# First tile of an FFN up projection: eight plain products instead of seven combined ones, with the combinations made meanwhile

## The chip, the cores and the metric

The kernel runs on one NeuronCore of one Trainium2 chip, as one program. Five engines have queues of their own: TensorE (PE in the profile; PEld are its weight loads), VectorE (DVE), ScalarE (ACT), GpSimd (POOL) and SyncE (SP, which here only issues DMAs). Each takes its instructions in a fixed order; semaphores make one wait for another. The metric is the time of one execution on the device in microseconds, median of several runs. Lower is better.

## What is computed

An encoder layer of width 1024 for 1024 "prompt" tokens and 256 "sample" tokens: a token mixing block, cross-attention into 256 memory tokens, and a gated feed-forward network (FFN), each with a root mean square norm in front and a residual sum behind. The change lies where the attention's output projection ends and the FFN begins:

```python
def rmsnorm(x, w):
    xf = x.astype(jnp.float32)
    y = xf * lax.rsqrt(jnp.mean(xf * xf, -1, keepdims=True) + EPS)
    return (y * w.astype(jnp.float32)).astype(x.dtype)
...
    return o @ w_o
...
    x = x + memory_cross_attention(rmsnorm(x, norm_xa_w), rmsnorm(mem, norm_mem_w), xa_w_q, xa_w_kv, xa_w_o)
    h = rmsnorm(x, norm_ffn_w)
    gu = h @ ffn_w_gate_up
    x = x + (jax.nn.silu(gu[..., :D_FF]) * gu[..., D_FF:]) @ ffn_w_down
```

Here D_FF is 2816, all tensors are float32.

## The kernel before

**Layout and precision.** Activations lie feature-major: 128 partitions, KT = 8 slices of features, tokens along the free dimension. Tokens form three blocks (`BLOCKS`): 0 and 1 are the prompt's halves of 512 tokens, 2 is the sample's 256. Every float32 product is made of three matmuls in the float32r type: `split` (line 124) writes a high part on ScalarE (line 125) and the remainder, the low part, on VectorE or GpSimd (line 126); `mm3` (line 110) issues high x high, high x low and low x high. So one 128-feature slice of a product costs three matmuls of 512 columns, or of 256 for the sample.

**Order of the work.** TensorE runs in the program's order, as the generators yield it. The other engines' instructions are ordered by the tile framework: by the order in the program and by when their inputs are ready, so that they may be placed well ahead of where the source has them; once built, each engine's order is fixed. Side jobs (`K.side`) are generators that wake when a clock has passed a due time. That clock is counted by hand in `mm` (line 100): a matmul of n columns adds n / 2.4 ns. A norm (`Norm.rest`, line 252) is such a job: after `lag` it sends a first few small matmuls (sums over partitions of the squares in `nacc`), then VectorE makes the inverse root (`nst`, lines 224 to 228), after `lag2` a few more small matmuls spread it, and then every `pace` one of 8 slices is scaled (line 284) and handed to a `sink`, which splits it.

**Output projection** (`OutProj.run`, line 1227). Eight weight tiles m, blocks b. Tiles 0 and 1 go first for all blocks, then block 0, 1 and 2 in turn with m = 2 to 7. `evac` (line 1237) adds the residual into x[b] and feeds the norm. After a block's last m its x is stored to `x2d`, and its norm is started as a side job. After block 0 `first_weights` loads the raw weights of the first up tile. The six weight tiles from m = 2 on lie in a pool of six rooms (`wx2`), closed when the projection ends.

**FFN up stage.** 22 tiles f of 128 gate and 128 up columns. For the prompt a seven-product (Strassen and Winograd) scheme is used for the pair gate and up over two halves of features and two halves of tokens. b11 and b21 are the feature halves of block 0, b12 and b22 of block 1. The combinations, made once and used by all tiles, are

    r1 = b11 - b12,  r2 = -b22 - r1,  t3 = b22 - b12,  t4 = -r2 - b21

and per tile four weight forms of 1024 columns: w(0) the gate weights, w(1) the first sums (`gu_sa`), w(2) the second sums (`gu_sb`), w(3) the up weights. A product, `gu_mm` (line 1570), is four slices, 12 matmuls of 512 columns. `sample` does the sample with plain weights in halves of 12 matmuls of 256 columns. `ff_up` (line 1757) is one tile: seven products, four half samples, gating, and stores for the down stage.

`ff_first` (line 1717) is tile 0. In it, block 1's sink has already formed r1 and r2 as the norm went along, slice by slice (lines 1427 and 1431); t3 and t4 are made between the products (`make_t3`, `make_t4`) in eight slices of 512 columns. Tile 0's combined weights are formed on VectorE within the projection. Tile 1's weights are loaded within `ff_first` (lines 1724 and 1741), two products of tile 1 are moved up into tile 0 to fill a gap, and block 2's norm is late (`LAGS` 19000, `LAGS2` 8000), so that the sample of tile 0 is done within tile 1.

## Time and profile before

| | |
|---|---|
| median of three runs | 2257.43 us (2254.76 to 2261.45) |
| the profiled execution | 2255.0 us |
| its span, first to last instruction | 2253.2 us |
| instructions in the trace | 32407 |
| matmuls, busy time of TensorE | 12468, 2196.2 us (97%) |
| VectorE, ScalarE, GpSimd busy | 1394.0, 815.5, 532.7 us |
| mean granted clock of TensorE | 0.993 |

Times in the profile's views are microseconds from the start of the span. Matmuls overlap, so the rate of TensorE is read from the distance of their starts. A wait is shown as the idle time of an engine ahead of an instruction, with the instruction whose end released it. "L284" is line 284 of the kernel; helpers such as line 126 serve many tiles, which the names before the arrow tell apart. In a groups row, after the bar, stand busy time, mean of one in ns, and idle time before them. In a waits row stand the total, how often, and the longest. In a windows row stand the length, then for each engine busy time and number of instructions, then the granted clock, the DMA share and the rate.

### The profile page before, as it was taken

To read this page: it belongs to the slowest core of one execution; us is meant where nothing else is said; L and a number is where in the kernel's file an instruction comes from. 1 tells how busy PE (TensorE), PEld (TensorE's weight loads), DVE (VectorE), ACT (ScalarE), POOL (GpSimd) and SP (SyncE) were. 2 spreads that over 40 slices of the span, in tenths; PEclk is the share of its full clock that TensorE was granted. 3 is DMA by queue.
4 is the path that set the end of the run, shared out by engine and by line. 5 is a ranking of instruction groups with operands and counts; after the bars stand their busy time and mean duration, and the time that the engine had idled before them with its cause. 6 is when DMAs were issued, how large, how long until landed. Compare 5 with 4: busy or idle time off the path is not lost.

```text
span 2253.2 us, 32407 instructions
## 1 busy us (share of the span) xinstructions
PE 2196.2 (97%) x12468; PEld 1918.3 (85%) x12468; DVE 1394.0 (62%) x2770; ACT 815.5 (36%) x1481; POOL 532.7 (24%) x355
## 2 busy tenths in 40 slices
PE   6999999999999999999999999899999999999998
PEld 6988888888888898888888888688888888888888
DVE  7768788887985964664534537544334334568575
ACT  5434243433424433233343423323232323243453
POOL 3010000000000000013231331565666566300031
PEclk9999999999999999999999999999999999999999
DMA  5221322223234445962231431223222222493531
GB/s 185 83 79 68 104 69 87 77 69 95 73 111 125 159 140 165 305 236 94 84 106 45 157 143 57 75 76 110 87 82 76 88 76 82 136 363 126 198 111 57
DMA packets 191301, 262.47 MB, mean 116 GB/s; under 512 B 72410, under 2 KB 102698, under 8 KB 191146
## 3 DMA queue, kind: packets, MB, share of 16 engines
q1 hardware_dynamic: 171306, 231.30, 30.9%
q10 hardware_dynamic: 19840, 29.11, 3.5%
q8 instruction: 97, 1.59, 0.3%
q14 instruction: 58, 0.48, 0.1%
HBM read 182.19 MB, written 78.16 MB: 116 GB/s over the span
## 4 chain that ended last, share of the span: by engine, by line
PE 82%; DVE 8%; issue 4%; DMA 2%; ACT 2%; POOL 1%; SPq 0%; POOLq 0%; ACTq 0%; DVEq 0%
PE bank L108 81%; PE bank L121 1%; DMA tbd<-stage 1%; DVE acc L599 1%; DVE wlo L126 1%; DMA t<-sgd 1%; DVE nt L284 1%; DVE U L845 0%; DVE sw L903 0%; DVE lo L126 0%; DMA stage<-gtd 0%; DVE W L745 0%; DVE nacc L249 0%; DVE aT L714 0%; DVE zt L837 0%
## 5 line engine op out<-in xcount | busy, mean ns | idle before, releaser
L108 PE MATMUL bank<-hi,whi 128*128 128x512 f32 (+1 forms) x2144 | 763.3, 356 | 2.8 <-ACT whi L125 1.7
L108 PE MATMUL bank<-lo,whi 128*128 128x512 f32 (+1 forms) x2144 | 748.8, 349 | 1.1 <-POOL lo L126 1.1
L108 PE MATMUL bank<-hi,wlo 128*128 128x512 f32 (+1 forms) x2144 | 748.3, 349 | 0.9 <-DVE wlo L126 0.9
L108 PEld LDWEIGHTS bank<-hi,wlo 128*128 128x128 f32 x2144 | 406.0, 189 | 54.9 <-DVE wlo L126 1.3
L108 PEld LDWEIGHTS bank<-hi,whi 128*128 128x128 f32 x2144 | 406.9, 190 | 52.7 <-ACT whi L125 2.2
L108 PEld LDWEIGHTS bank<-lo,whi 128*128 128x128 f32 x2144 | 407.1, 190 | 49.8 <-POOL lo L126 1.4
L126 POOL TENSOR_TENSOR wlo<-raw,whi 128x1024 fp32r<-128x1024 f32 x70 | 177.8, 2542 | 377.2 <-ACT whi L125 377.2
L125 ACT ACTIVATE whi<-raw 128x1024 fp32r<-128x1024 f32 (+1 forms) x141 | 144.5, 1026 | 195.3 <-PE bank L108 146.9
L126 POOL TENSOR_TENSOR wlo<-room,whi 128x1024 fp32r<-128x1024 f32 x42 | 100.6, 2396 | 115.7 <-ACT whi L125 115.7
L108 PE MATMUL bank<-bhl,whi 128*128 128x512 f32 x408 | 125.7, 389 | 0.0
L126 DVE TENSOR_TENSOR wlo<-raw,whi 128x1024 fp32r<-128x1024 f32 (+1 forms) x71 | 82.3, 1159 | 43.6 <-ACT whi L125 41.5
L125 ACT ACTIVATE whi<-room 128x1024 fp32r<-128x1024 f32 x42 | 44.6, 1061 | 142.5 <-PE bank L108 138.6
L1796 DVE TENSOR_TENSOR room<-room,bank 128x512 f32<-128x512 f32 x21 | 14.5, 688 | 131.8 <-ACT room L1567 131.8
L108 PEld LDWEIGHTS bank<-bhl,whi 128*128 128x128 f32 x408 | 76.5, 188 | 15.9
L599 DVE SCALAR_TENSOR_TENSOR acc<-craw,sm,acc 128x510 f32<-128x510 f32 (+1 forms) x96 | 73.6, 766 | 20.5 <-ACT acc L597 19.0
L108 PE MATMUL bank<-bhl,wlo 128*128 128x512 f32 x204 | 79.5, 390 | 1.2 <-DVE wlo L126 1.2
L745 DVE TENSOR_TENSOR W<-W,UT 128x2 f32<-128x2 f32 (+30 forms) x155 | 73.2, 472 | 10.1 <-DMA W<-in_eye 5.8
L248 ACT ACTIVATE nsq<-x 128x512 f32<-128x512 f32 (+1 forms) x70 | 40.2, 583 | 102.7 <-DVE x L1237 92.4
L962 ACT ACTIVATE gs<-bank 128x512 f32<-128x512 f32 (+1 forms) x60 | 31.2, 520 | 125.2 <-PE bank L108 119.9
L1589 DVE SCALAR_TENSOR_TENSOR t<-bank,t 128x512 f32<-128x512 f32 (+1 forms) x44 | 24.6, 558 | 82.2 <-PE bank L108 82.2
L249 DVE TENSOR_TENSOR nacc<-nacc,nsq 128x512 f32<-128x512 f32 (+1 forms) x72 | 54.4, 755 | 33.2 <-ACT nsq L248 31.9
L108 PE MATMUL bank<-bhl,ahl 128*128 128x512 f32 x312 | 73.8, 392 | 0.0
(345 smaller groups left out, 4223.1 us busy)
## 6 DMA issues: line engine op xcount, KB each, us to landing
raw<-in_w_gu SPq DMA_DIRECT2D x44, 512.0 KB, 3.9
braw<-gq SPq DMA_DIRECT2D x14, 1024.0 KB, 5.4
raw<-in_w_g SPq DMA_DIRECT2D x20, 512.0 KB, 3.3
gq<-t SPq DMA_DIRECT2D x33, 256.0 KB, 2.0
gtd<-gs ACTq DMA_DIRECT2D x32, 256.0 KB, 2.0
w<-in_w_dn SPq DMA_DIRECT2D x8, 1024.0 KB, 11.9
raw<-in_w_qkv SPq DMA_DIRECT2D x12, 512.0 KB, 3.6
gq<-r SPq DMA_DIRECT2D x22, 256.0 KB, 4.3
```

The lines of the kernel that those rows point to most:

```text
L108: self.nc.tensor.matmul(out, l, r, start=start, stop=stop, skip_group_check=more)
L121: self.nc.tensor.transpose(out, x, ident)
L125: self.nc.scalar.activation(hi, src, AF.Copy)
L126: (eng or self.nc.vector).tensor_tensor(out=lo, in0=src, in1=f32(hi), op=ALU.subtract)
L248: S.activation(sq, x, AF.Square)
L249: (eng or V).tensor_tensor(out=self.acc, in0=self.acc, in1=sq, op=ALU.add)
L284: V.scalar_tensor_tensor(out=t, in0=xk(k), scalar=sm[:, wcol + k : wcol + k + 1], in1=pb[:, :n], op0=ALU.mult, op1=ALU.mult)
L599: V.scalar_tensor_tensor(out=dst, in0=src, scalar=wj, in1=dst, op0=ALU.mult, op1=ALU.add)
L745: V.tensor_tensor(out=t3, in0=u3[:, i:, c:].rearrange("p j c -> p c j"), in1=XL[:, 32 * i + i : 32 * i + 32].unsqueeze(1).to_broadcast([P, ...
L962: S.activation(t, ps, AF.Tanh, scale=0.5)
L1589: V.scalar_tensor_tensor(out=out, in0=u, scalar=sign, in1=t, op0=ALU.mult, op1=ALU.mult)
L1796: V.tensor_tensor(out=c22, in0=c22, in1=pe, op=ALU.add)
```

## The change

- Tile 0 no longer uses the seven-product scheme. Gate and up are each made by four plain products (b11, b21 for block 0; b22, b12 for block 1): eight products. The copies and sums that put the seven products together go.
- Tile 0's sample is done at the end of tile 0, and tile 1 becomes an ordinary tile.
- Block 1's sink only splits. Its slices come in the order 4 to 7, 0 to 3; slices 0 to 3 (b12) go to rooms of their own. `PACES` and `LAGS2` set the pace of each block's slices (600, 1300, 600) and the second lag (2800, 9500, 7000); the first lag is 1500 for all.
- r1, r2, t3 and t4 are made during the plain products, in operations on two slices (1024 columns) at a time.
- The rooms of the projection's weights m = 2 to 7 are reused one by one as its last block goes (`after(m)`): tile 1's gate and up weights, then b12 (later t3), then r2.
- Tile 1's raw weights are loaded during the projection, after tile 0's were split; its sums are made in place on GpSimd after m = 3 of the last block.
- In all tiles the gate and up weights keep one fixed room each, and the two sums rotate in the two rooms of `wp`.

The core of the diff:

```diff
+                    if b == 2 and after is not None:
+                        after(m)
...
-                if sinks is None or b == 2:
-                    norm_b = nms[b].rest(xk, wcol, to_h(hs, b), 600, lag=1500 if sinks is None else LAGS, inplace=sinks is not None, ready=ready, lag2=2800 if sinks is None else LAGS2)
+                if sinks is None:
+                    norm_b = nms[b].rest(xk, wcol, to_h(hs, b), 600)
                 else:
-                    norm_b = nms[b].rest(xk, wcol, sinks(b, x, hs), (600, PACE1)[b], inplace=True)
+                    norm_b = nms[b].rest(xk, wcol, sinks(b, hs), PACES[b], ks=range(KT) if b != 1 else SECOND_KS, inplace=True, lag2=LAGS2[b])
...
+    SECOND_KS = (4, 5, 6, 7, 0, 1, 2, 3)
...
         def sink(k, t):
-            if k < 4:
-                V.tensor_tensor(out=x0[:, k, :], in0=x0[:, k, :], in1=t, op=ALU.subtract)
-                split(hi[:, k, :], lo[:, k, :], x0[:, k, :], V)
-            else:
-                r2_raw.append(bank())
-                V.scalar_tensor_tensor(out=r2_raw[k - 4], in0=t, scalar=-1.0, in1=x0[:, k - 4, :], op0=ALU.mult, op1=ALU.subtract)
-                split(hi[:, k, :], lo[:, k, :], t, V)
+            h, l = (b12[0][:, k, :], b12[1][:, k, :]) if k < 4 else (hi[:, k, :], lo[:, k, :])
+            split(h, l, t, V)
...
     def gu_gate(f, eng=G):
         if f < NFF:
-            gu_w[f, 0] = pair_of(wp)
+            gu_w[f, 0] = gu_w[1, 0]
...
+        if f == 1:
+            split(hi[:, :512], lo[:, :512], g[:, :512], V)
+            split(hi[:, 512:], lo[:, 512:], u[:, 512:], V)
+            return
...
-        gu_w[f, 2] = pair_of(tpool)
+        hi, lo = gu_w[f, 2] = pair_of(wp)
...
     def gu_up(f):
-        gu_w[f, 3] = pair_of(tpool)
+        gu_w[f, 3] = gu_w[1, 3]
...
+        def splits():
             yield FIRST_W
...
+            for i in (0, 3):
+                gu_w[0, i] = pair_of(wp)
+                split(*gu_w[0, i], gu_raw[0][i // 3], G)
+            gu_load(1, wp)
...
+    def after(m):
+        room = tuple(tpool.tile([P, 1024], F32R, tag=t, name=t) for t in ("whi", "wlo"))
+        if m > 3:
+            for x, t in zip(b12 if m < 6 else r2, room):
+                x.parts.append(t.rearrange("p (k t) -> p k t", t=512))
+            return
+        gu_w[1, 0 if m == 2 else 3] = room
+        split(*room, gu_raw[1][m - 2], G)
+        if m == 3:
+
+            g, u = gu_raw[1]
+            for x, y in ((u[:, 512:], u[:, :512]), (u[:, :512], g[:, :512]), (g[:, :512], u[:, 512:]), (g[:, 512:], g[:, :512])):
+                G.tensor_tensor(out=x, in0=x, in1=y, op=ALU.add)
...
+    def make_r1():
+        for i in (0, 2):
+            V.tensor_tensor(out=room[:, i : i + 2, :], in0=room[:, i : i + 2, :], in1=x1[:, i : i + 2, :], op=ALU.subtract)
+        parts(r1, room)
+
+    def make_r2():
+
+        for i in (0, 2):
+            a, b = x1[:, i : i + 2, :], x1[:, 4 + i : 6 + i, :]
+            V.tensor_tensor(out=a, in0=b, in1=a, op=ALU.subtract)
+            V.scalar_tensor_tensor(out=b, in0=b, scalar=-1.0, in1=room[:, i : i + 2, :], op0=ALU.mult, op1=ALU.subtract)
+        parts(r2, x1[:, 4:, :])
+
+    def make_t34():
+        nonlocal fp
+        for i in (0, 2):
+            x = room[:, 4 + i : 6 + i, :]
+            V.scalar_tensor_tensor(out=x, in0=x1[:, 4 + i : 6 + i, :], scalar=-1.0, in1=x, op0=ALU.mult, op1=ALU.subtract)
+        parts(t3, x1)
         xhs.close()
...
+        parts(t4, room[:, 4:, :])
...
+        gate, up_ = gu_w[0, 0], gu_w[0, 3]
+        pa, pu, pb, pv = (bank(pm) for _ in range(4))
+        for ps, w in ((pa, gate), (pu, up_)):
+            yield from gu_mm(ps, w, 0, b11, True)
+            yield from gu_mm(ps, w, 1, b21, False)
+            if ps is pa:
+                t1 = silu2(pa)
+        times_up(t1, pu, store1(0), 1.0)
+        K.finish(K.pending.pop((id(h3), 1)))
+        yield from gu_mm(pb, gate, 1, b22, True)
+        yield from gu_mm(pb, gate, 0, b12, False)
+        t2 = silu2(pb)
+        make_r1()
+        yield from gu_mm(pv, up_, 1, b22, True)
+        yield from gu_mm(pv, up_, 0, b12, False)
+        c22 = ff(x2p, "nacc", "c22", bufs=2)
+        times_up(t2, pv, store2(0), 1.0, c22)
+        make_r2()
+        K.finish(K.pending.pop((id(h3), 2)))
+        smp.extend(half(h3[2], i) for i in range(2))
+        sg, su = (bank()[:, :NS] for _ in range(2))
+        yield from sample(sg, gate, (0, 1))
+        gu_sa(1)
+        ts_ = silu2(sg, NS)
+        make_t34()
+        yield from sample(su, up_, (0, 1))
+        times_up(ts_, su, gsd[0], 1.0)
         pending["last"] = 0, t1, c22
...
-LAGS, LAGS2, FIRST_W = 19000, 8000, 9000
-PACE1 = 1900
+FIRST_W, PACES, LAGS2 = 9000, (600, 1300, 600), (2800, 9500, 7000)
```

More of the change, by code (lines that the diff above doesn't have):

```diff
@@ L1225, in begin, with run @@
                 yield from self.parts(m, b, range(KT - 2))
-        def run(self, xsrc, scale, wcol, xpool, store, sinks=None, then=None, ready=None):
+        def run(self, xsrc, scale, wcol, xpool, store, sinks=None, then=None, after=None):
             ps = (xpool,) * 3 if sinks is None else (x0p, xhp, xpool)
@@ L1561, in sum_room, with copied @@
         return room[:, i : i + 2, :].rearrange("p a b -> p (a b)")
-    def copied(ps, t=None):
+    def copied(ps, t=None, first=False):
         if t is None:
             turns["p"] += 1
-            t = room[:, 4 + turns["p"] % 2, :]
+            t = room[:, (0 if first else 4) + turns["p"] % 2, :]
         S.activation(t, ps, AF.Copy)
@@ L1717, in ff_first @@
     def ff_first():
-        w = lambda i: gu_w[0, i]
-        pb, pf, pe, pa = (bank(pm) for _ in range(4))
-        cs = first_copies
-        raw = K.raw()[:, :1024]
-        SY.dma_start(raw, a["w_gu"][1])
-        gu_raw[1] = [raw]
-        yield from gu_mm(pb, w(0), 1, b21, True)
-        yield from gu_mm(pa, w(0), 0, b11, True)
-        p1 = copied(pa, cs[:, 0, :])
-        t1 = gate_of(pb, p1)
-        yield from gu_mm(pe, w(1), 1, r1, True)
-        yield from gu_mm(pa, w(1), 0, r2, False)
@@ L1732, in ff_first @@
-        gu_gate(1, V)
-        make_t3()
-        yield from gu_mm(pf, w(2), 1, b22, True)
-        u2 = copied(pa, cs[:, 1, :])
-        V.tensor_tensor(out=u2, in0=u2, in1=pe, op=ALU.add)
-        t2 = gate_of(pf, u2)
-        make_t4()
-        split(*gu_w[0, 3], gu_raw[0][1], V)
-        raw = K.raw()[:, :1024]
-        SY.dma_start(raw, a["w_gu"][NFF + 1])
-        gu_raw[1].append(raw)
-        make_room()
-        pn = bank(pm)
-        yield from gu_mm(pn, gu_w[1, 0], 0, b11, True)
-        pn2 = bank(pm)
@@ L1747, in ff_first @@
-        first_out.extend((pn, pn2))
-        yield from gu_mm(pn2, gu_w[1, 0], 1, b21, True)
-        yield from gu_mm(pa, w(2), 0, t3, False)
-        c22 = copied(pa, second_block(0))
-        V.tensor_tensor(out=c22, in0=c22, in1=pe, op=ALU.add)
-        times_up(t2, c22, store2(0), -1.0, c22)
-        yield from gu_mm(pa, w(3), 1, t4, False)
-        times_up(t1, pa, store1(0), -1.0)
+        gate, up_ = gu_w[0, 0], gu_w[0, 3]
[5 more added lines that the diff above has]
+                t1 = silu2(pa)
@@ L1759, in ff_up @@
         second, last = f == 1, f == NFF - 1
-        sums = lambda: (bank()[:, :NS], bank()[:, :NS])
-        if second:
-            pa, pb = first_out
-            p1 = copied(pa)
-            t1 = gate_of(pb, p1)
-            combine(*pending["last"])
-            K.finish(K.pending.pop((id(h3), 2)))
-            smp.extend(half(h3[2], i) for i in range(2))
-            sg0, su0 = sums()
-            yield from sample(sg0, gu_w[0, 0], (0, 1))
-            gu_sa(1)
-            ts0 = silu2(sg0, NS)
-            sg, su = sums()
-            yield from sample(su0, gu_w[0, 3], (0, 1))
-            times_up(ts0, su0, gsd[0], 1.0)
-        else:
-            pa, pb = bank(pm), bank(pm)
-            yield from gu_mm(pa, w(0), 0, b11, True)
-            p1 = copied(pa)
-            sg, su = sums()
-            yield from sample(sg, w(0), (0,))
-            yield from gu_mm(pb, w(0), 1, b21, True)
-            t1 = gate_of(pb, p1)
-            combine(*pending["last"])
+        pa, pb = bank(pm), bank(pm)
+        yield from gu_mm(pa, w(0), 0, b11, True)
+        p1 = copied(pa, None, second)
+        sg, su = (bank()[:, :NS] for _ in range(2))
+        yield from sample(sg, w(0), (0,))
+        yield from gu_mm(pb, w(0), 1, b21, True)
+        t1 = gate_of(pb, p1)
+        combine(*pending["last"])
         gu_sb(f)
         gu_load(f + 1, wp if f % 2 == 0 else x2p)
-        yield from sample(sg, w(0), (0, 1) if second else (1,))
+        yield from sample(sg, w(0), (1,))
         yield from gu_mm(pa, w(1), 0, r2, False)
-        u2 = copied(pa)
-        gu_up(f)
+        u2 = copied(pa, None, second)
+        if not second:
+            gu_up(f)
         if last:
```

77 lines of the change are left out of this document (25 added, 52 removed).

## Prediction

> **What bounds the kernel now.** I read the page first. The profiled execution took 2255.0 us, of which the span is 2253.2, so 1.8 us lie around it; the three timed runs have a median of 2257.43, which is 2.4 above. The sum below is made against 2255.0 and then carried over to 2257.4.
>
> ```profile
> span 2253.2 us, 32407 instructions
> PE 2196.2 (97%) x12468; PEld 1918.3 (85%) x12468; DVE 1394.0 (62%) x2770; ACT 815.5 (36%) x1481; POOL 532.7 (24%) x355
> ...
> raw<-in_w_gu SPq DMA_DIRECT2D x44, 512.0 KB, 3.9
> ```
>
> TensorE is busy 97% of the span: a change pays only where TensorE waits, and costs wherever it adds matmuls. So I looked next for the waits of TensorE in the stretch that the diff touches. It begins where the output projection has issued its last product (1397.52 us, below called Z) and ends where up tile 2 starts (1464.04 us). The waits view for TensorE over exactly that stretch:
>
> ```profile
> PE bank L108 <- DVE nst L228: 4.3, 1, 4.3
> PE bank L108 <- ACT whi L125: 1.7, 1, 1.7
> PE bank L108 <- POOL lo L126: 1.1, 1, 1.1
> PE bank L108 <- ACT hi L125: 1.0, 1, 1.0
> PE bank L108 <- DVE wlo L126: 0.9, 1, 0.9
> PE bank L108 <- DVE r2l L126: 0.8, 1, 0.8
> PE bank L108 <- ACT room L1567: 0.7, 1, 0.7
> PE bank L108 <- DVE x L1547: 0.6, 1, 0.6
> ```
>
> These add up to 11.1 us, and all are waits for operands being prepared: nst is the third token block's normalisation, whi and wlo are tile 1's gate weights, r2l a combination of activations. The windows view shows the same by tens of us:
>
> ```profile
> core 0: us, PE busy (x) PEld busy (x) DVE busy (x) ACT busy (x) POOL busy (x), PEclk, DMA share, GB/s
> 1378.08:1397.52 19.44, 19.26 (x161) 19.08 (x160) 14.65 (x36) 5.64 (x12) 0.00 (x0) 1.00 0.29 109
> 1397.52:1464.04 66.52, 55.45 (x274) 45.92 (x273) 41.55 (x77) 27.00 (x45) 30.08 (x20) 0.92 0.23 79
> ...
> 1410.00:1420.00 10.00, 6.77 (x30) 4.76 (x30) 10.00 (x17) 6.08 (x10) 0.00 (x0) 1.00 0.14 52
> ...
> 1430.00:1440.00 10.00, 4.76 (x19) 4.17 (x20) 8.31 (x16) 4.27 (x9) 8.16 (x7) 0.54 0.33 105
> ```
>
> In 1410 to 1420 VectorE is busy all of the 10 us while TensorE works 6.77: VectorE limits there. In 1430 to 1440 TensorE is down to 4.76 and the granted clock to 0.54, so after the 4.3 us wait the matmuls also run slowly for a while.
>
> **What the stretch would take without waits.** From the groups by form and the timeline of TensorE:
>
> ```profile
> L108 PE MATMUL bank<-hi,whi 128*128 128x512 f32 x32 | 12.7, 397 | 1.7 <-ACT whi L125 1.7
> ...
> L108 PE MATMUL bank<-hi,whi 128*128 128x256 f32 x32 | 10.1, 317 | 1.0 <-ACT hi L125 1.0
> ```
>
> ```profile
> 1397.52 0.40 PE L108 MATMUL bank<-hi,whi 128*128 128x512 f32 x1
> ...
> 1409.54 0.39 PE L108 MATMUL bank<-hi,whi 128*128 128x512 f32 x1
> ...
> 1412.03 0.39 PE L108 MATMUL bank<-hi,wlo 128*128 128x512 f32 x1
> ...
> 1441.45 0.28 PE L108 MATMUL bank<-lo,whi 128*128 128x256 f32 x1
> ...
> 1447.33 0.28 PE L108 MATMUL bank<-hi,wlo 128*128 128x256 f32 x1
> ...
> 1464.04 0.39 PE L108 MATMUL bank<-hi,whi 128*128 128x512 f32 x1
> ```
>
> The starts, not the durations, give the rate, since matmuls overlap. 1409.54 and 1412.03 are the first and the last of the 12 matmuls of one product: 2.49 / 11 = 0.227 us each, 2.72 us a product. 1441.45 to 1447.33 spans 49 steps of 256 columns: 0.12 us each, 1.44 us for a half sample (12 matmuls). In this stretch the code has 14 products (seven for each of tiles 0 and 1) and 8 half samples: 38.1 + 11.5 = 49.6 us. The third block's norm puts 4 + 4 small matmuls in: the stretch before (first row of the windows, 19.44 us) has 144 steps of 0.12, 17.3 us, and 16 such small ones, so 2.1 / 2 = 1.0 us for eight. So 50.6 of 66.5 us are work, and 15.9 us are lost: the 11.1 of waits, the slow clock, and refilling after each wait.
>
> **The change, part by part.** *TensorE.* Tile 0 takes eight products for seven: +2.72 us, on the path. All else stays: 15 products, 8 half samples, the norm's matmuls, 40.8 + 11.5 + 1.0 = 53.3 us. If no wait were left the stretch would gain 66.5 - 53.3 = 13.2 us. This is the ceiling.
>
> *Waits that go.* Tile 1's gate and up weights are loaded in the second block's products and split from the third block's on; the gate's 1.7 and 0.9 go. The two loads (3.9 us each) move ahead of Z on SP's queue, past the second block's store, which stands behind them; their cover is the second block, 144 matmuls of 0.227 or 32.7 us, in place of two waits for them. Tile 1's sums go from after 1426 to POOL before Z. The first eight products need only plain activations: block 1's have been ready long before Z, so 4 products, 10.9 us, run with nothing to wait for; then b22 and b12, due at Z + 10.9 and Z + 13.6. Block 2's norm is scaled from 1.5 + 9.5 us on the schedule after its last product, where block 3 takes 15.4 (144 times 256 / 2.4 ns); so it begins 4.4 before Z there, 4.9 at the trace's 0.12.
>
> *The third block's norm.* It moves from 19 us after its last product to the default 1.5, and its second half from 8.0 to 7.0 later. It thereby gets new waits: TensorE takes instructions in order, so behind the norm's first matmul all the plain products queue. That matmul needs the last sum of squares:
>
> ```profile
> 1379.73 0.69 DVE L249 TENSOR_TENSOR nacc<-nacc,nsq 128x512 f32<-128x512 f32 x1 [0.76 <-ACT nsq L248]
> ...
> 1401.06 0.42 DVE L249 TENSOR_TENSOR nacc<-nacc,nsq 128x256 f32<-128x256 f32 x1
> ...
> 1424.57 0.16 DVE L266 TENSOR_SCALAR bank<-bank 128x2 f32<-128x2 f32 x1
> ...
> 1432.96 0.15 DVE L228 SCALAR_TENSOR_TENSOR nst<-bank,nst 128x2 f32<-128x2 f32 x1
> ```
>
> With VectorE full (second row) the sum stood 4.0 us after its block's last product at 1397.5; with VectorE idle (first row; products ended 1378.1) 2.3 us. It will be asked for at about 1.6 us (the schedule counts 512 / 2.4 ns = 0.213 us a matmul where the trace has 0.227, so its 1.5 is 1.6 and its 7.0 is 7.4): a wait of 0.7 to 2.4. VectorE will be busy with block 2 again, but with two operations a slice, no longer three: I take 1.7. The chain to nst took 8.5 us between the last two rows, among long operations; it now has 7.4 us, and block 2's last slices are through by about Z + 8, after which nothing urgent is in its way: 0 to 4.3, and I take 0.3.
>
> *VectorE.* Prices, from the groups by form between 1340 and 1470 (the last three are POOL's):
>
> ```profile
> L284 DVE SCALAR_TENSOR_TENSOR x<-x,sm,bank 128x512 f32<-128x512 f32 x16 | 11.3, 741 | 0.0
> L126 DVE TENSOR_TENSOR lo<-x,hi 128x512 fp32r<-128x512 f32 x12 | 9.2, 770 | 0.9 <-ACT hi L125 0.9
> ...
> L126 DVE TENSOR_TENSOR wlo<-raw,whi 128x1024 fp32r<-128x1024 f32 x3 | 3.7, 1218 | 0.0
> L284 DVE SCALAR_TENSOR_TENSOR x<-x,sm,bank 128x256 f32<-128x256 f32 x8 | 3.4, 473 | 1.3 <-PE bank L108 1.3
> ```
>
> ```profile
> L126 POOL TENSOR_TENSOR wlo<-raw,whi 128x1024 fp32r<-128x1024 f32 x10 | 24.9, 2491 | 32.6 <-ACT whi L125 32.6
> ...
> L1475 POOL TENSOR_TENSOR room<-raw 128x512 f32<-128x512 f32 x3 | 4.1, 1382 | 63.5 <-DMA raw<-in_w_gu 63.5
> ...
> L126 POOL TENSOR_TENSOR lo<-x,hi 128x256 fp32r<-128x256 f32 x4 | 3.4, 882 | 0.0
> ```
>
> Due before tile 1's second kind of product (r2): block 2's norm 8 x (0.74 + 0.77) = 12.1; block 3's 12 x 0.47 = 5.7; its chain of eleven at 0.16, 1.8; the last two evacuations with their sums, 4 at 0.42, 1.7; gating of tiles 0 and 1, sums of weights and one combination, 9 x 0.74 + 2 x 0.47 = 7.6; r1 four and r2 six wide operations at 1.22, 12.2. Sum 41.1 us. It may start at Z - 4.9 and is due after 10 products, 6 half samples and the norm, Z + 36.9, or Z + 38.9 with the 2.0 of waits: 43.8 us, 2.7 to spare. The t3 that follows wants 4 wide ones and a half sum, 5.6 us, where TensorE gives 5.4, so what is late for r2 stays late once, not twice. POOL can eat the spare:
>
> ```profile
> 1467.93 2.86 POOL L126 TENSOR_TENSOR wlo<-raw,whi 128x1024 fp32r<-128x1024 f32 x1
> ```
>
> ```profile
> 1468.56 2.78 DVE L1618 SCALAR_TENSOR_TENSOR r<-r,room 128x512 f32<-128x512 f32 x1
> ```
>
> A VectorE operation of 0.74 took 2.78 beside a POOL one, and ended 0.55 after it: it was held until POOL was done. POOL's work for tile 1 (two splits of 2.49, four sums of 1.38, 10.5 us) has the 14 us before Z; its tail may reach past Z - 4.9, and four small splits of block 3 follow. I take 1.2 us of lateness, of 0 to 8.7 (see the first rival).
>
> [...]
>
> *The end of the up stage.* The sums of weights now rotate through the rooms in which gate and first sum rotated. In the last tile, the second room for the down stage's operand 1 is therefore read until the last product; before it was free three products earlier.
>
> ```profile
> 1970.19 2.31 DVE L126 TENSOR_TENSOR wlo<-araw,whi 128x1024 fp32r<-128x1024 f32 x1
> ```
>
> ```profile
> 1972.56 0.50 PE L108 MATMUL bank<-bhl,wlo 128*128 128x512 f32 x1 [1.21 <-DVE wlo L126]
> ```
>
> VectorE already makes TensorE wait 1.21 there, and gets one more wide operation (1.22) ahead of it: 0 to 2.4, I take 0.7. Tiles 2 to 20 have the same rooms' life and no TensorE wait now: nothing.
>
> **Sum.** Stretch 53.3 + 1.7 + 0.3 + 1.2 = 56.5 against 66.5: -10.0; down +0.7; net -9.3. 2255.0 becomes 2245.7, and the median 2257.4 becomes 2248.1.
>
> **Rivals.** *VectorE becomes the bound (0.22).* If all of POOL's work that can fall in the window, four sums 5.5, one split 2.5 and block 3's four 3.4, holds VectorE off, then 11.4 us less the 2.7 to spare are 8.7 us late: stretch 53.3 + 2.0 + 8.7 = 64.0, net -1.8, 2255.6. For it: the two rows above. Against it: most of POOL's work lies where VectorE has gaps, and the L284 operations (one input in PSUM, 741 ns even among POOL's) are not held.
>
> *The wait for nst only moves (0.12).* The norm of block 3 now falls in VectorE's busiest part. With 2.4 + 4.3 us and the slow clock again, the first 18 of its half-sample matmuls at 0.21 for 0.12 (1.8), it is 8.5 instead of 2.0: net -2.8, 2254.6. Here the wait of 1.7 in 1410 to 1420 left the clock at 1.00 and the one of 4.3 did not.
>
> [...]
>
> *Slower (0.08).* If VectorE is held off for 13 us between Z - 5 and Z + 45, nothing is gained (13.2 - 2.0 - 0.7 + 2.7 = 13.2), and from 20 us on a loss is seen. Of its two-input operations there, 8 lo slices, 16 wide ones and 4 halves of sums, each would have to lose about 1 us: 28 - 2.7 + 2.0 + 0.7 - 13.2, or +15 us, 2272. It needs POOL at work in most of that stretch, where it has 11.4 us by count.
>
> **How the numbers follow.** A measurement of this kernel tells about 0.3% (6.8 us) from no change. The forecast has 0.58 with its own range 2244 to 2251, the ends being no wait at all (-13.2) and nearly double the waits (-6). Some 0.05 of it, above 2250.6, counts as no change, and some 0.07 of the two rivals with 0.34 comes out better than -6.8: faster 0.58 - 0.05 + 0.07 = 0.60, same 0.34 - 0.07 + 0.05 = 0.32, slower 0.08. The range for 8 in 10 goes from 0.7 below the ceiling's 2244.2, for the scatter of a median, to just past the first rival: 2243.5 to 2256.
>
> **What would show it.** In the profile after: stretch from the last projection product to tile 2 of 55 to 58 us; 12 more matmuls; no TensorE wait for whi, wlo or t4's source there; one of 1 to 2 us for nacc soon after Z; granted clock 1.00 throughout. Wrong would be: a wait for nst of over 3 us with a clock near half (second rival); waits for r2l, t3l or lo with two-input VectorE operations of 2 us and more (first and third); a gap at 1970 longer by over 2 us; or any new wait before Z.

## The result and the profile after

The changed kernel took 2241.66 us (median of four runs, 2239.54 to 2244.17) beside 2256.1 us for the kernel before (four runs, 2252.9 to 2261.45): a ratio of 0.9934, 95% interval 0.9911 to 0.9957, so faster by 0.66%. Timed again in five rounds beside fifteen runs of the kernel before (first experiment) it took 2243.14 against 2255.67, a ratio of 0.9943, interval 0.993 to 0.9957. The forecast was 2248.1 with a range from 2243.5: faster as foretold, but by 14.4 and 12.5 us where 9.3 were forecast, and the first median lies 1.8 below the range, the second 0.4.

The profiled execution took 2244.17 us. Its page begins:

```profile
span 2242.3 us, 32397 instructions
...
PE 2195.8 (98%) x12480; PEld 1920.4 (86%) x12480; DVE 1394.7 (62%) x2749; ACT 813.2 (36%) x1473; POOL 531.5 (24%) x355
```

There are twelve matmuls more than before, as the eighth product costs, and still a shorter span. In the windows the first row is the stretch from the projection's last product (Z, now 1398.52) to up tile 2, the others the two stretches of 10 us that showed the trouble before:

```profile
core 0: us, PE busy (x) PEld busy (x) DVE busy (x) ACT busy (x) POOL busy (x), PEclk, DMA share, GB/s
...
1398.52:1453.58 55.06, 53.72 (x287) 46.13 (x285) 44.73 (x69) 24.97 (x38) 16.91 (x12) 1.00 0.22 77
1410.00:1420.00 10.00, 9.26 (x43) 7.77 (x44) 10.00 (x19) 4.90 (x10) 3.05 (x4) 1.00 0.10 31
...
1430.00:1440.00 10.00, 10.00 (x57) 8.74 (x56) 10.00 (x13) 4.63 (x7) 1.79 (x1) 1.00 0.27 92
```

The stretch takes 55.06 us, from 66.52. VectorE is as full as before, or fuller (10.00 in both), but TensorE works on at a granted clock of 1.00. All of TensorE's waits in that stretch are now one line of the waits view:

```profile
PE bank L108 <- DVE nst L228: 1.3, 1, 1.3
```

The rest of the span hardly moved. In both traces 479.14 us lie between the t4 product of tile 2 and the first matmul of the down stage; the first 300 matmuls of the down stage took 69.25 us after and 69.71 before. So the two profiled executions differ by -11.5 in the stretch, -0.5 at the down stage and +1.0 ahead of Z, in a part that the change doesn't touch.

### The profile page after: what moved, and what is told of

The parts are those of the page before. It is cut to its first block, busy times and chain, and to the rows that moved or that the text cites. A ratio compares the mean times of both kernels' runs of the same rounds, so it can differ in the third digit from the quotient of the medians.

```text
span 2242.3 us, 32397 instructions
## 1 busy us (share of the span) xinstructions
PE 2195.8 (98%) x12480; PEld 1920.4 (86%) x12480; DVE 1394.7 (62%) x2749; ACT 813.2 (36%) x1473; POOL 531.5 (24%) x355
## 4 chain that ended last, share of the span: by engine, by line
PE 82%; DVE 7%; issue 5%; DMA 3%; ACT 2%; POOL 1%; SPq 0%; ACTq 0%; POOLq 0%; DVEq 0%
PE bank L108 81%; DMA tbd<-stage 1%; PE bank L121 1%; DVE acc L599 1%; DVE wlo L126 1%; DVE nt L284 1%; DVE sw L903 0%; DMA gb<-grd 0%; DVE U L845 0%; DMA yod<-gs 0%; DVE lo L126 0%; DMA stage<-gtd 0%; DVE nacc L249 0%; DVE aT L714 0%; DMA t<-sgd 0%
## 5 line engine op out<-in xcount | busy, mean ns | idle before, releaser
L126 POOL TENSOR_TENSOR wlo<-x,whi 128x1024 fp32r<-128x1024 f32 x40 | 96.5, 2411 | 48.1 <-ACT whi L125 48.1
L1791 DVE TENSOR_TENSOR x<-x,bank 128x512 f32<-128x512 f32 x21 | 14.5, 689 | 126.1 <-ACT x L1586 126.1
L249 DVE TENSOR_TENSOR nacc<-nacc,nsq 128x512 f32<-128x512 f32 (+1 forms) x72 | 59.8, 831 | 35.7 <-ACT nsq L248 34.4
L1599 DVE SCALAR_TENSOR_TENSOR t<-t,x 128x512 f32<-128x512 f32 x42 | 64.0, 1523 | 28.4 <-ACT t L1598 28.4
L745 DVE TENSOR_TENSOR W<-W,UT 128x2 f32<-128x2 f32 (+30 forms) x155 | 73.0, 471 | 10.9 <-DMA W<-in_eye 6.6
L125 ACT ACTIVATE whi<-x 128x1024 fp32r<-128x1024 f32 (+1 forms) x48 | 49.0, 1026 | 79.8 <-PE bank L108 73.6
## 6 DMA issues: line engine op xcount, KB each, us to landing
w<-in_w_dn SPq DMA_DIRECT2D x8, 1024.0 KB, 11.5
```

The lines of the kernel that those rows point to most:

```text
L125: self.nc.scalar.activation(hi, src, AF.Copy)
L126: (eng or self.nc.vector).tensor_tensor(out=lo, in0=src, in1=f32(hi), op=ALU.subtract)
L249: (eng or V).tensor_tensor(out=self.acc, in0=self.acc, in1=sq, op=ALU.add)
L745: V.tensor_tensor(out=t3, in0=u3[:, i:, c:].rearrange("p j c -> p c j"), in1=XL[:, 32 * i + i : 32 * i + 32].unsqueeze(1).to_broadcast([P, ...
L1599: V.scalar_tensor_tensor(out=t, in0=t, scalar=1.0, in1=src, op0=ALU.add, op1=ALU.mult)
```

## The experiments

The measure in most of them is the stretch from Z to tile 2, read from each run's windows. Two traces of the changed kernel agree in it to 0.06 us, two of the kernel before, where the clock fell, only to 1.2; so where the clock in the table is under 1.00, a single trace tells about a microsecond. Every kernel is the changed one with the edit shown, unless it says otherwise. The third token block, the sample's, is block 2 of the code; what the prediction calls block 2 and block 3 are the code's blocks 1 and 2. The sum of TensorE's waits is from the waits view; the clock is the stretch's.

| run | stretch us | waits us | clock |
|---|---|---|---|
| before, first and second trace | 66.52, 67.71 | 11.1, 10.2 | 0.92, 0.90 |
| after, first and second trace | 55.06, 55.00 | 1.3, 1.3 | 1.00 |
| norm_9000 | 53.47 | 0 | 1.00 |
| norm_1500 | 61.79 | 6.8 | 0.94 |
| slices | 54.41 | 0.3 | 1.00 |
| products_2 | 60.46 | 1.3 | 1.00 |
| dve_4 | 57.82 | 3.8 | 1.00 |
| dve_8 | 68.16 | 11.1 | 0.90 |
| cover_quarter | 56.78 | 5.4 | 0.94 |
| cover_half | 57.85 | 11.0 | 0.88 |
| dve_4_sb | 56.53 | 2.5 | 1.00 |
| cover_quarter_sb | 49.91 | 1.3 | 1.00 |
| pool_5 | 62.14 | 5.6 | 0.95 |
| before_lag15 | 69.20 | 12.3 | 0.90 |

**Both kernels again.** after_again and before_again are the two kernels without an edit.

> The changed kernel unchanged, timed again in more rounds, and a second trace of it. Scatter theory (the 3 us by which the medians differ more than the two profiled executions lie ahead of the changed part): the stretch from the last projection product to tile 2 takes 55.1 us again, within 0.3, the one TensorE wait in it is for nst, 1.3 us; the ratio comes out nearer to 0.9952 (the profiled executions, 2244.17 / 2255.0) than to 0.9936 (the medians). Rival: the change also gains about 3 us outside the marked stretches, and the ratio stays at 0.9936 or below.

> The kernel before, unchanged, for a second trace. Scatter theory: from the last projection product to tile 2 again 66.5 us, with the same waits within 0.3 us, from the fourth product of tile 2 to the down stage 479.1, and what differs from the first trace lies ahead of the last projection product, up to some 5 us. Rival: the stretch itself scatters by 2 us or more, and the comparison of single traces is worth as little as that.

The stretch after was 55.00, with the same one wait, and the ratio 0.9943. Before, it was not steady: 67.71, 1.2 us more than in the first trace. The waits are as long as they were, within 0.3 us, and one of 0.6 is gone; the clock differs. These are rows of the second trace's windows; the first trace has 1.00 throughout from 1408 to 1428:

```profile
1415.00:1420.00 5.00, 3.90 (x11) 2.81 (x11) 5.00 (x9) 2.09 (x5) 0.00 (x0) 0.70 0.00 0
1420.00:1425.00 5.00, 5.00 (x25) 4.24 (x24) 5.00 (x8) 2.27 (x4) 0.00 (x0) 0.96 0.00 0
```

So the kernel before paid a varying price for its waits, and the kernel after had none that cost clock in its two traces. With the mean of before's two stretches, 67.1, the change is worth 12.1 us there, which is nearly all of the 12.5 by which the second pair of medians differs. What is ahead of Z scatters too, in all runs and whatever the kernel: Z came between 1394.57 and 1401.41.

**What the wait for nst is worth, and its size.** The second lag of the third block's norm, both ways:

```diff
-FIRST_W, PACES, LAGS2 = 9000, (600, 1300, 600), (2800, 9500, 7000)
+FIRST_W, PACES, LAGS2 = 9000, (600, 1300, 600), (2800, 9500, 9000)
```

with 1500 in the place of 9000 in norm_1500.

> The second lag of the third block's norm from 7000 to 9000 on the schedule's clock (2.1 us at the trace's rate of 0.227 us a matmul). Theory (TensorE bounds the stretch, the wait of 1.3 us for nst is all that is left of the waits): the wait goes, the stretch takes 53.7 instead of 55.1 us, the time falls by 1.3 to 1.5 us; the third block's slices are scaled 0.8 us later and its sample, 8 products after Z, does not wait. VectorE-bound rival: VectorE's order is full, so the later norm moves its slices into the combinations, and r2 or the sample wait by about 1 us: no gain.

> The second lag of the third block's norm from 7000 to 1500 (5.9 us earlier at the trace's rate): TensorE then asks for nst 5.9 us before it does now. In-order theory: the plain products queue behind that matmul, so TensorE waits 1.3 + 5.9 = 7.2 us; with the clock as before the change (a wait of 4.3 us was followed by matmuls of 0.21 for 0.12 us and a clock of 0.54) some 2 us more: +6 to +8 us. If the slow clock comes with any wait of that length, the windows after it show a granted clock near half for some us. Rival (VectorE bounds the stretch): the wait only takes the place of a later one for r2, and the time changes by less than 3 us.

norm_9000 has no wait of TensorE left in the stretch, which takes 53.47 us: the prediction counted 53.3 us of work. Its time was 2241.27 us (five runs), a ratio to before of 0.9939, interval 0.9926 to 0.9952, against 0.9943 for the changed kernel on the same chip. The trace shows the gain of 1.5 us; the times agree with it but can't prove it. Its stretch is the shortest here of a kernel that computes the whole layer.

norm_1500 asks 24 matmuls earlier, 5.4 us, and waits 5.5 longer:

```profile
PE bank L108 <- DVE nst L228: 6.8, 1, 6.8
```

```profile
1403.00:1408.00 5.00, 0.00 (x0) 0.00 (x0) 5.00 (x12) 2.32 (x3) 0.00 (x0) 0.75 0.00 0
1408.00:1413.00 5.00, 3.54 (x12) 3.06 (x13) 4.70 (x9) 2.02 (x4) 0.00 (x0) 0.56 0.01 3
```

The stretch is 6.7 longer: 5.5 of wait and 1.2 of slow clock (0.56 in the second row). Nothing later took the wait's place. In time it is 2251.18 against 2243.14, 8.0 us. TensorE's order is what counts here: whatever it meets too early, everything queues behind.

**Whether TensorE is the bound.** products_2 issues two plain products twice; slices makes the combinations in operations half as wide.

```diff
         yield from gu_mm(pb, gate, 1, b22, True)
+        yield from gu_mm(pb, gate, 1, b22, True)
...
         yield from gu_mm(pv, up_, 1, b22, True)
+        yield from gu_mm(pv, up_, 1, b22, True)
```

```diff
-        for i in (0, 2):
-            V.tensor_tensor(out=room[:, i : i + 2, :], in0=room[:, i : i + 2, :], in1=x1[:, i : i + 2, :], op=ALU.subtract)
+        for i in range(4):
+            V.tensor_tensor(out=room[:, i, :], in0=room[:, i, :], in1=x1[:, i, :], op=ALU.subtract)
```

(and so for r2, t3, t4 and their splits).

> The changed kernel with two plain products more, b22's of gate and of up issued twice (so block 1 of tile 0 gets that half twice, a changed computation): TensorE gets 24 more matmuls at 0.227, 5.44 us. Theory (TensorE bounds the stretch): 5.4 us more, 60.5, the wait for nst still 1.3 us. VectorE-bound rival: TensorE's extra work falls into what would be waits, 0 to 3 us more.

> The changed kernel with r1, r2, t3 and t4 made in operations of 512 columns, one slice each, instead of 1024 (the sums on VectorE, the high parts on ScalarE, the low parts on VectorE). An operation of 512 columns took 0.74 us, one of 1024 took 1.22, so each of the ten VectorE operations due before r2's product costs 0.26 more, 2.6 us in all, and the six of t3 and t4 1.6. Theory (TensorE bounds the stretch; in the changed kernel's trace the last low part of r2 ends at 1430.9 where its product starts at 1436.8, so VectorE has 5.9 us to spare): no new wait, the stretch stays at 55.0 us, within 0.3. VectorE-bound rival: 2.6 us longer, with a wait of about that for r2l.

products_2 took 60.46, 5.40 more for 5.44 us of matmuls: TensorE's work counts in full. (The second of each pair starts its bank anew, so the results are those of one.) slices gave VectorE 1.43 us more busy time (4.2 were reckoned) and the stretch became 0.65 shorter: the wait for nst fell from 1.3 to 0.3. These rows of the changed kernel's trace, and below them those of slices, say why:

```profile
1407.43 1.22 DVE L1551 TENSOR_TENSOR x<-x,x 128x1024 f32<-128x1024 f32 x1
...
1409.23 0.16 DVE L227 TENSOR_TENSOR bank<-bank,nst 128x2 f32<-128x2 f32 x1
1409.30 1.22 DVE L1551 TENSOR_TENSOR x<-x,x 128x1024 f32<-128x1024 f32 x1
1410.44 0.15 DVE L228 SCALAR_TENSOR_TENSOR nst<-bank,nst 128x2 f32<-128x2 f32 x1
...
1410.74 0.68 PE L108 MATMUL bank<-cst,nst 128*128 128x128 f32 x4 [1.34 <-DVE nst L228]
```

```profile
1406.00 0.68 DVE L1551 TENSOR_TENSOR x<-x,x 128x512 f32<-128x512 f32 x1
...
1407.40 0.68 DVE L1551 TENSOR_TENSOR x<-x,x 128x512 f32<-128x512 f32 x1
```

Two wide operations of r1 stand between links of the norm's chain, the second ahead of the last link, for which TensorE waits. In slices two of 0.68 us stand at the same places, and the chain is 1.0 us shorter, 7.8 for 8.8. A wide operation saves VectorE time (1.22 us for two slices, where two of 0.68 take 1.36), and it is also a longer block in front of whatever small thing is due.

**How far behind VectorE is.** dve_8 computes the low parts of r1 and r2 three times, dve_4 those of r2 alone:

```diff
             split(h, l, src[:, i : i + 2, :], V)
+            for _ in range(2 * (hl is r1 or hl is r2)):
+                V.tensor_tensor(out=l, in0=src[:, i : i + 2, :], in1=f32(h), op=ALU.subtract)
```

> The changed kernel with eight more wide operations on VectorE: each of the four low parts of r1 and r2 is computed three times instead of once, 8 x 1.22 = 9.8 us. Theory (5.9 us to spare ahead of r2's product): 9.8 - 5.9 = 3.9 us of wait, the stretch 58 to 60 us, the wait before r2's product or, since four of the eight stand ahead of the third block's slices, in part before the sample of tile 0. VectorE-bound rival: the whole 9.8, stretch 65. TensorE-only rival (VectorE is not near to binding): no change, 55.

> The changed kernel with four more wide operations on VectorE, the two low parts of r2 computed three times each, 4 x 1.22 = 4.9 us, or 4.5 by the distance of their starts. Theory, mended after eight such operations cost 13.1 us (waits for t3's low part and for the low part of tile 1's second sums, none for r2): VectorE has spare time up to the product of t3, 7.9 us (its low part ends at 1434.5 where its product starts at 1442.4), and GpSimd's sums, which stood 7.35 us beside a VectorE without gaps, add what they lose: 4.5 us are covered, the stretch stays at 55.0, at most 56. Rival (VectorE bound, each operation costs its length or, as with eight, more): 60 to 62.

Both expectations failed. Eight operations cost 13.1 us, more than their own length (9.8 of it are waits, the rest went with a slow clock, 0.50 in 1448 to 1458), and four cost 2.8. r2 waited in neither. (The 1430.9 that dve_8's expectation takes for r2's low part is that of tile 1's first sums, the other operand of the same product; r2's own ended at 1429.7, and the product began at 1437.0.) The wait of dve_4 is this one, for the low part of tile 1's second sums, the weights that t3 is multiplied by:

```profile
1448.40 0.50 PE L108 MATMUL bank<-whi,wlo 128*128 128x512 f32 x1 [2.49 <-DVE wlo L126]
```

Its place in VectorE's order is what differs. In the changed kernel the first half of that split (wlo<-raw) stands ahead of t4's low parts, in dve_4 behind them:

```profile
1435.46 0.68 DVE L126 TENSOR_TENSOR wlo<-raw,whi 128x512 fp32r<-128x512 f32 x1
1436.06 2.35 DVE L126 TENSOR_TENSOR t4l<-x,t4h 128x1024 fp32r<-128x1024 f32 x2
```

```profile
1444.80 2.35 DVE L126 TENSOR_TENSOR t4l<-x,t4h 128x1024 fp32r<-128x1024 f32 x2
...
1447.67 2.37 DVE L126 TENSOR_TENSOR wlo<-raw,whi 128x512 fp32r<-128x512 f32 x2
```

The framework fixes each engine's order when the kernel is built, so an operation added in one place moves others past each other. In dve_8 the same split stands behind t4 too (7.8 us of wait, after one of 2.0 for t3's low part), and VectorE and GpSimd hold each other up: an operation of GpSimd that took 1.30 in the changed kernel took 7.35 beside a VectorE without a gap, and two of VectorE's, 1.2 each, took 5.65 beside GpSimd:

```profile
1430.73 7.35 POOL L1468 TENSOR_TENSOR x<-raw 128x512 f32<-128x512 f32 x1 [12.38 <-DVE x L1561]
...
1439.09 5.65 DVE L1568 SCALAR_TENSOR_TENSOR x<-x,x 128x1024 f32<-128x1024 f32 x2
```

**Whether the plain products are needed as cover.** cover_half leaves out block 1's four products, cover_quarter the two of its up half. The edit of cover_quarter:

```diff
-        yield from gu_mm(pv, up_, 1, b22, True)
-        yield from gu_mm(pv, up_, 0, b12, False)
         c22 = ff(x2p, "nacc", "c22", bufs=2)
-        times_up(t2, pv, store2(0), 1.0, c22)
+        times_up(t2, pu, store2(0), 1.0, c22)
```

> The changed kernel without the four plain products of block 1 (their results are left out: t2 and c22 are made from block 0's instead, so that VectorE and ScalarE do the same work). TensorE loses 4 x 2.72 = 10.9 us of work, and with it of cover. Theory: the sample of tile 0 is asked for 10.9 us earlier, at about 13 us after the last projection product, where the third block's last slices are scaled 18 us after it, and r2's product is asked for before its low part is there by 10.9 - 5.9 = 5.0 us; the same VectorE order stands behind both, so waits of 4 to 6 us in all appear, and the stretch is 10.9 - 5 = about 6 us shorter, 48 to 51 us. If the plain products were no cover (TensorE-only rival): no wait appears, 44 us. VectorE-bound rival: all of the 10.9 becomes wait, 55 us.

> The changed kernel without the two plain products of block 1's up half (left out: c22 is made from block 0's up half, so VectorE and ScalarE work as before), 5.44 us of TensorE work. Theory (spare time ahead of the sample about 4 us, ahead of r2 5.9): the stretch is 4 to 5.4 us shorter, 49.6 to 51, with waits of at most 1.5 us. Rival (plain products are needed in full as cover, as four of them were: without those the stretch was 2.8 us longer): 55 or more, with waits for the sample's or r2's operands of 5 us and over.

Neither became faster: with 10.9 us of work less the stretch is 2.8 longer, with 5.4 less it is 1.7 longer. My 48 to 51 for the first and 49.6 to 51 for the second were wrong, and the rivals' 55 was nearer. cover_half's waits view:

```profile
PE bank L108 <- ACT hi L125: 7.6, 2, 6.6
PE bank L108 <- POOL lo L126: 2.5, 2, 1.3
PE bank L108 <- DVE nst L228: 0.9, 1, 0.9
```

hi and lo are the sample's parts. In that build the last slices of the third block are scaled behind r2's wide sums on VectorE, where the changed kernel has them ahead:

```profile
1419.11 2.35 DVE L1559 SCALAR_TENSOR_TENSOR x<-x,x 128x1024 f32<-128x1024 f32 x2
...
1424.05 1.25 DVE L284 SCALAR_TENSOR_TENSOR x<-x,sm,bank 128x256 f32<-128x256 f32 x3
```

So the order had changed here too; whether the four products could be left out in a better order was not tried. cover_quarter waits 2.9 us for ScalarE's copy of a bank and 1.2 for the low part of the second sums, which again stands behind t4:

```profile
PE bank L108 <- ACT x L1586: 2.9, 1, 2.9
...
PE bank L108 <- DVE wlo L126: 1.2, 1, 1.2
```

**Work or order.** After these four VectorE looked like a second bound just behind TensorE. The other reading is that it has the time and that the waits come from the place of one split. dve_4_sb and cover_quarter_sb are the two kernels with that split moved ahead of t3 and t4:

```diff
-        make_t34()
         yield from sample(su, up_, (0, 1))
         times_up(ts_, su, gsd[0], 1.0)
+        gu_sb(1)
+        make_t34()
...
-        gu_sb(f)
+        if not second:
+            gu_sb(f)
```

> The kernel with four more wide operations on VectorE (4.5 us), and with the split of tile 1's second sums placed ahead of t3 and t4 in VectorE's order; with the four alone it stood behind t4, TensorE waited 2.5 us for its low part and the stretch took 57.8. Order theory (VectorE has the time, and the wait came from the place of that split in a fixed order): t3's low part moves back by two splits, 1.2 us, from 1442.0 to 1443.2, with its product due at 1445.3; no wait but nst's 1.3, the stretch 55.0 to 55.5. Work theory (VectorE's sum of work is the bound): the wait of 2.5 us turns into one for t3's low part, the stretch stays at 57 to 58.

> The kernel without the two plain products of block 1's up half (left out: c22 is made from block 0's), and with the split of tile 1's second sums ahead of t3 and t4 in VectorE's order. Without that move the stretch took 56.8 us: 5.4 us of TensorE work less, and waits of 2.9 (ScalarE's copy of a bank, behind its high parts of t3) and 1.2 us (the split's low part) with a slow clock after them. Order theory: both waits come from the order, so they go for the larger part, the stretch takes 50 to 53. Work theory (without the cover VectorE is the bound): a wait of 3 us and more for t3's parts takes their place, 55 to 57.

cover_quarter_sb took 49.91 us, 6.9 less than without the move and 5.15 less than the changed kernel, for 5.44 us of matmuls left out. The one wait left is the old one:

```profile
PE bank L108 <- DVE nst L228: 1.3, 1, 1.3
```

That is the order theory's end, and it contradicts the work theory: the same VectorE work, with 5.4 us less to cover it, makes no new wait. dve_4_sb went part of the way: the wait for the split is gone, none came for t3, but 1.2 us remain for ScalarE's copy of a bank, so 1.5 of the 2.8 are left. ScalarE's rows say where that copy (L1588, in cover_quarter_sb L1586) stands: in dve_4_sb behind t4's high parts, as in cover_quarter, and in cover_quarter_sb ahead of them. In the changed kernel it stands behind them too, but there they begin 36.2 us after Z, in dve_4_sb 42.2 (Z is 1394.57).

```profile
1436.78 2.01 ACT L125 ACTIVATE t4h<-x 128x1024 fp32r<-128x1024 f32 x2 [2.66 <-DVE wlo L126]
...
1439.21 0.58 ACT L1588 ACTIVATE x<-bank 128x512 f32<-128x512 f32 x1
```

```profile
1432.80 0.60 ACT L1586 ACTIVATE x<-bank 128x512 f32<-128x512 f32 x1 [1.80 <-PE bank L108]
1436.80 2.01 ACT L125 ACTIVATE t4h<-x 128x1024 fp32r<-128x1024 f32 x2 [3.40 <-DVE wlo L126]
```

(The expectation of cover_quarter_sb calls them t3's high parts; the rows are t4's.) So in dve_4_sb the later t4 does reach TensorE, by way of ScalarE's order. And in cover_quarter_sb moving the split moved an operation of ScalarE too, so the 6.9 us belong to both places together. Moving the copy alone was not tried.

**Two rivals by themselves.** pool_5 gives GpSimd five wide operations beside VectorE's full stretch; before_lag15 is the kernel before with only the third block's norm earlier.

```diff
         times_up(t1, pu, store1(0), 1.0)
+        for i in (0, 2, 0, 2, 0):
+            G.tensor_tensor(out=b21[1][:, i : i + 2, :], in0=room[:, 4 + i : 6 + i, :], in1=f32(b21[0][:, i : i + 2, :]), op=ALU.subtract)
```

```diff
-LAGS, LAGS2, FIRST_W = 19000, 8000, 9000
+LAGS, LAGS2, FIRST_W = 15000, 8000, 9000
```

> The changed kernel with five more operations of 1024 columns on GpSimd (b21's low part formed again, the same values) behind the first product's gating, 5 x 2.4 = 12 us beside VectorE's full stretch. First rival's mechanism (a VectorE operation with two inputs in SBUF and one of GpSimd hold each other off): VectorE loses up to 12 us, less the 5.9 to spare ahead of r2's product: the stretch 55 to 61 us, with VectorE operations of 2 us and more that took 1.22, and GpSimd's of more than 2.4. Without such a hold: stretch 55.0, the GpSimd operations 2.4 us each, VectorE's unchanged.

> The kernel before with the first lag of the third block's norm 15000 instead of 19000, and nothing else of the change: the norm begins 4 us earlier. Rival (the gain comes from the earlier norm): the wait of 4.3 us for nst and the slow clock after it go, 6 to 8 us of the change's 12. Theory (VectorE's order is full until the combinations are through, and the cover of plain products is what the change gains by): the norm's chain of small VectorE operations is earlier by what little the order leaves, the time falls by 0 to 4 us, and waits for r2l, t3's parts or the sample grow in its place.

pool_5 took 62.14, 7.1 more, a little above the first rival's 61. The timeline of VectorE, and GpSimd's five in one row:

```profile
1406.01 2.85 DVE L126 TENSOR_TENSOR wlo<-x,whi 128x512 fp32r<-128x512 f32 x1
...
1408.85 3.28 DVE L1551 TENSOR_TENSOR x<-x,x 128x1024 f32<-128x1024 f32 x1
1412.06 0.15 DVE L228 SCALAR_TENSOR_TENSOR nst<-bank,nst 128x2 f32<-128x2 f32 x1
1412.13 3.31 DVE L126 TENSOR_TENSOR lo<-x,hi 128x1024 fp32r<-128x1024 f32 x1
1415.36 0.86 DVE L284 SCALAR_TENSOR_TENSOR x<-x,sm,bank 128x256 f32<-128x256 f32 x2
...
1405.95 14.28 POOL L1747 TENSOR_TENSOR lo<-x,hi 128x1024 fp32r<-128x1024 f32 x5 [13.12 <-PE bank L108]
```

An operation of 0.69 took 2.85, two of 1.22 took 3.28 and 3.31; L284, which reads a bank and one tile, took its usual 0.86 for two. The hold is real. But the price did not come by way of r2, as the rival had it: held operations stand in the norm's chain, the wait for nst grew from 1.3 to 5.6, and with the slow clock beside it (0.68 in 1408 to 1418) the stretch lost 2.8 more.

before_lag15 was slower, not faster: a ratio of 1.0016 to before, interval 1.0006 to 1.0025 (ten runs), with a stretch of 69.20.

```profile
PE bank L108 <- DVE x L1547: 7.9, 1, 7.9
```

TensorE asks for the norm 4 us earlier and then stands 7.9 us behind the operation that forms t4 out of a bank; before, it stood 0.6 there. That the norm's matmul waits for a bank which r2's raw sums still hold is how the names read; it was not tried by itself. So the early norm brings nothing alone. That it needs combinations that no longer sit in banks, and products to issue meanwhile, is argued from these rows: the other parts of the change were not tried one by one. My 0 to 4 us of gain were wrong in sign.

## Where the prediction was right, and which step failed

**Right.** The work of the stretch: 53.3 us counted, 53.47 measured in norm_9000, without a wait. The waits that went: those for tile 1's weights, r2l, t4's source and the sample's parts are all gone. The clock: 1.00 in the stretch. The mechanism holds in this: TensorE's waits went, at the price of one product that counts in full (products_2). That the plain products are needed as cover is shown only in part. Without two of the eight no wait came once the order was right (cover_quarter_sb), so those two are no cover that the kernel needs; without four, in an order left as it fell, 11.0 us of waits came.

**The step that failed** is the range's low end, "0.7 below the ceiling's 2244.2, for the scatter of a median". No size of the waits could have reached what was measured, since with all of them at nothing the sum ends at 2244.2. What it stands on was wrong: the base, 2257.43, taken as if it were known to 0.7 us, and the ceiling's gain of 13.2, from one trace. The base was a median of three runs 6.7 us apart, and the next medians of the same kernel were 2256.1, 2255.67 (fifteen runs) and 2255.51 (thirteen). Those of the changed kernel were 2241.66 and 2243.14. The medians of three and of four lay 1.5 to 1.9 us from the later ones, once in the base and once in what is measured. From 2255.67 the same sum gives 2246.4 and a ceiling of 2242.5; the second median, 2243.14, lies 0.7 above that ceiling, as fits a kernel with 1.3 us of waits. In the sum itself the terms for waits were too large: 1.7 + 0.3 + 1.2 = 3.2 us in the stretch, where it is 1.6 longer than without a wait (55.06 against norm_9000's 53.47), and 0.7 at the down stage, where half of the traces show less than before.

**Sizes that were off**, all but that of nst to the side of too long a time:

- The wait for nacc, taken at 1.7, is 0. The sum stood at 2.5 us after Z, within the bounds of 2.3 to 4.0. But it was asked for at 2.75, not at 1.6, as these rows of the changed kernel show: Z is 1398.52, and the norm's first matmul comes behind a whole product of 12.

```profile
1400.57 0.42 DVE L249 TENSOR_TENSOR nacc<-nacc,nsq 128x256 f32<-128x256 f32 x1
...
1401.27 0.50 PE L108 MATMUL bank<-cst,nacc 128*128 128x1 f32 x4
```

A side job comes in between slices of three matmuls only, and its lag counts from the first such point (`pump` adds it to the clock of that moment): 1500 on the clock are a little over 7 matmuls, and after the first 3 that makes a little over 10, so the 12th. The second lag gave 9, 33 and 45 matmuls for 1500, 7000 and 9000, each rounded up to whole slices.
- The wait for nst, taken at 0.3, is 1.3. From the norm's first matmul (1401.27) to the end of nst (1410.59) went 9.3 us, and TensorE was through with the 33 matmuls between 7.9 after it. The 8.5 expected were read from VectorE's first link on and left out the 0.5 ahead of that; and of the 8.8 that it took from there, 2.4 are r1's two wide operations, where the prediction saw nothing urgent in the way.
- VectorE's lateness at r2, taken at 1.2 with 2.7 to spare, is 0. r2's low part stood 7.3 us ahead of its product, the low part of the first sums 6.1. What POOL was feared to take, it did not, since its sums for tile 1 were done before Z. The last of them, and the first matmul of r2's product:

```profile
1394.12 1.36 POOL L1531 TENSOR_TENSOR raw<-raw 128x512 f32<-128x512 f32 x1
...
1436.98 0.40 PE L108 MATMUL bank<-whi 128*128 128x512 f32 x1
```

- The down stage, taken at +0.7, was -0.5 in two of the four timed kernels' traces and +0.7 or +0.8 in the other two (300 matmuls in 69.25, 69.25, 70.42 and 70.49 us beside 69.71): the same code, with a second wait of 0.7 to 0.8 us in some executions. The wait that was to grow there, 1.21, fell to 0.53 in all four.
- The gain itself was read from one trace of before, 66.52; the second has 67.71.

Stretch 55.06 for 56.5, down -0.5 for +0.7, base 2255.67 for 2257.43: that is 1.4 + 1.2 + 1.8 of the 6.4 us between 2248.1 and 2241.66; 1.5 more is the distance of the two medians after. (The trace of the second median's run has +0.8 for the down stage, so this adds up single runs and is no more than a rough account.)

**The rivals.** The first (VectorE held off by POOL) has its mechanism confirmed by pool_5. It is at work in the changed kernel too, where a half split of 0.68 us takes 2.30, but at places where TensorE did not wait for it:

```profile
1438.21 2.47 POOL L126 TENSOR_TENSOR wlo<-raw,whi 128x1024 fp32r<-128x1024 f32 x1 [10.76 <-ACT whi L125]
```

```profile
1438.93 2.30 DVE L126 TENSOR_TENSOR wlo<-raw,whi 128x512 fp32r<-128x512 f32 x1
```

In pool_5's rows the operations that read two tiles took 3.28 and 3.31 for 1.22, and the L284 pair, which reads a bank and one tile, an unchanged 0.86. The second (nst with a slow clock) is what norm_1500 shows, at 6.7 us; with the lag as chosen the wait stayed at 1.3. (Its 1.8 us for 18 matmuls at 0.21 for 0.12 come to 1.6.) The third (slower) did not come near: it would have taken VectorE 20 us of hold.

## What to carry to other kernels

Before adding up an engine's spare time, look at which operand stands where in its fixed order: here the same VectorE work made 2.9 and 1.2 us of wait or none, by the place of one split and of a ScalarE copy that moved with it. Work that needs only what has long been ready can be worth its price on the bounding engine if it covers the preparation of the rest, but how much of it is needed shows only once the order is right: two of the eight products were not. The norm's early start alone was worth nothing. And where a base is a median of three runs 7 us apart, that scatter belongs to the range, once for the base and once for the result.

## What was not expected of the hardware

The clock fell without any long wait in the second trace of before: 0.70 in 1415 to 1420, where the longest wait of TensorE was 1.9 us with one of 0.7 close behind it, and 1.00 in the first trace with 1.7 and 0.9. Waits of 1.3 and 2.5 us alone left it at 1.00 (the changed kernel, dve_4); after waits of 4.3, 5.6, 6.8 and 7.8 us, and in cover_quarter after one of 2.9 with one of 1.2 behind it, it was between 0.50 and 0.68. The row of pool_5, with the wait of 5.6 in it, and that of dve_8 from the middle of the 7.8 on:

```profile
1408.00:1418.00 10.00, 5.65 (x15) 4.66 (x16) 10.00 (x10) 1.87 (x3) 9.64 (x5) 0.68 0.04 14
```

```profile
1448.00:1458.00 10.00, 3.79 (x9) 3.02 (x10) 8.16 (x7) 2.82 (x5) 4.39 (x2) 0.50 0.34 113
```

The wait alone does not tell it in the two traces of before; how it lies in time differs. In them the clock changes at edges a multiple of 3.41 us apart: half clock lasted 3.41 us in the second trace (1417.03 to 1420.44) and 10.24 in the first (1430.90 to 1441.14). Cut at these edges, the second trace reads as in the first two rows, the first trace with nearly the same waits as in the next two, and around its wait of 4.3 us as in the last two:

```profile
1413.61:1417.03 3.42, 0.94 (x3) 0.50 (x4) 3.42 (x6) 2.10 (x3) 0.00 (x0) 1.00 0.00 1
1417.03:1420.44 3.41, 3.41 (x11) 2.76 (x10) 3.41 (x7) 1.18 (x3) 0.00 (x0) 0.50 0.00 0
```

```profile
1410.42:1413.83 3.41, 2.00 (x9) 1.31 (x7) 3.41 (x6) 2.56 (x4) 0.00 (x0) 1.00 0.40 154
1413.83:1417.25 3.42, 2.22 (x8) 1.53 (x9) 3.42 (x6) 1.41 (x3) 0.00 (x0) 1.00 0.00 0
```

```profile
1427.49:1430.90 3.41, 1.39 (x6) 0.77 (x5) 2.77 (x7) 0.63 (x1) 3.33 (x4) 1.00 0.00 0
1430.90:1441.14 10.24, 5.90 (x24) 5.31 (x25) 7.41 (x16) 4.27 (x9) 7.34 (x6) 0.50 0.36 114
```

In one execution both waits fall, but for 0.12 us, into one piece, in the other an edge cuts through the longer one. TensorE was busy, as the profile counts it, for 0.94 of the 3.42 us ahead of half clock in the second trace (0.27) and for 1.39 of 3.41 in the first (0.41); the two pieces of the first with 2.00 and 2.22 us (0.59 and 0.65) were followed by full clock. This is what these four pieces show and no limit for every kernel.

GpSimd was held up for long beside VectorE too: in dve_8 7.35 us for an operation that took 1.30 in the changed kernel, while VectorE went from one operation to the next without a gap (10.00 of 10.00 us busy in 1428 to 1438).
